# The states' keys through GpSimd's queue, and a start in which two blocks of tokens take the weights as they arrive

## The chip, the cores and the metric

The kernel runs on one core of a Trainium2 chip. The metric is the device time of one execution in microseconds (us), as the median of several runs. The core has five engines with a queue of instructions each: TensorE (PE, matrix products; its weight loads are shown apart as PEld), VectorE (DVE), ScalarE (ACT), GpSimd (POOL) and SyncE (SP), which here issues transfers only. ACT and POOL issue transfers too. An engine works through its queue in order; engines wait for each other by semaphores. Products go to PSUM, which has eight banks of 128 x 512 float32 values; everything else lies in SBUF or in memory.

## The reference, cut to what matters

One decoder layer on 1024 tokens of width 1024, all in float32:

```
xn   = rms_norm(x) * norm_mix_g
proj = xn @ w_in        # [sb_q, sb_k, sb_v, g_q, g_k, g_v, g_r, g_a, gate_sb, gate_gla]
o_sb  = stick_breaking_attention(sb_q, sb_k, sb_v)          # 8 heads x 64
o_gla = gla_chunked(g_q, g_k, g_v, log_a)                   # 4 heads, d_k 64, d_v 128
y = sigmoid(gate_sb + b0) * (o_sb @ w_branch_sb) + sigmoid(gate_gla + b1) * (o_gla' @ w_branch_gla)
h = x + y @ w_out
h = h + conv_ffn(rms_norm(h))                               # gated, causal convolution, width 2816
out = rms_norm(h) * norm_final_g
```

Two places concern the change. The first is the norm with the projection to `sb_v` (columns 1024 to 1535 of `w_in`), which is the first matrix product of the kernel. The second is the gated linear attention, whose state after each chunk is a sum of products of decayed keys with values:

```
k_to_end = kf * exp(cum_last - cum)
d_state  = einsum('bhnck,bhncv->bhnkv', k_to_end, vf)
state    = dec * state + d_state
```

## The kernel before, in words

Tokens are taken in eight blocks of 128 (`NT`), the width in eight pieces of 128 (`NK`). To keep float32's precision at a faster product, an operand is split into a high part (a cast to `fp32r` on ACT) and a low part (a subtraction on DVE); `split` (L118) does both, and a product of two operands is three products: high by high, low by high, high by low. `piece` (L180) splits a 128 x 512 piece of weights into one buffer.

Buffers come from rings: `t8` (16 of 8 KB a partition), `t4` (14 of 4 KB), `t2` (11 of 2 KB) and `bank` (the eight of PSUM). A new tile waits until an earlier one of its ring is given back. The program's order is a proposal: a planner puts the instructions of each engine into an order by their place in the program and by when it takes their operands and buffers to be ready. A dependency without a semaphore, added by hand (`add_manual_dep`), holds two instructions of one engine in an order.

**The start.** SP loads the first block of x (L383), the norm's factors broadcast to all 128 partitions (L396, 512 KB), then the weights of `sb_v` in four loads of two 128-row pieces each (L173), with the next blocks of x between them. `normed(0)` squares, scales (L310 to L313) and transposes (L321) block 0 and splits it; then the eight weight pieces are split; then for each block in turn `value` (L360) makes its 24 products (L367), copies the result (L372) and stores it (L373), while `normed` prepares the next block.

**The end of attention.** `attend` (L724) goes through the heads; its products (L677, L691) are mixed with steps of the gates' projection (`gates`, L555; products by `mac`, L197). `gather` (L706, products L712) finishes a head's two token blocks, its result goes to memory by SP (L720) and is loaded again by SP in `fetch_heads` (L702), added and split. After the loop `branch(0, ...)` (L910) is started: its first step loads the first weights of `w_branch_sb` and splits two pieces. Four steps of the gates follow (`BEFORE`, L991), then `fetch_rest` (L794) loads the decayed keys `kt_d`, which the kernel had stored earlier, in two loads of 512 KB on SP (L800), then the rest of the gates. Then `gated` (L885) runs the linear attention: `states` (L803) makes a product per chunk and pair of heads (L808), DVE adds it to the state (L815, L817) and POOL scales it (L819). Steps of `branch(0)`, which multiply the attention's rows by the branch's weights (`mac`, L197) and by the gates loaded on SP (L930), are set between them.

Of the kernel before, what the change touches and what calls it, by code (L numbers as in the profile page):

```python
# [34 lines left out]
C_GATE = 3088  # L35
T2 = 11
T4 = 14
FILL = 6, 4
# [10 lines left out]
FFN_FROM = 18  # L49
BEFORE = 4  # L50
PAIR_SKEW = 3
# [14 lines left out]
def block_kernel(ctx: ExitStack, tc: tile.TileContext, x, norm_mix_g, w_in, b_gate, w_alpha_up, b_alpha,  # L66
# [51 lines left out]
    def split(h, l, src):  # L118
        nc.scalar.copy(h, src)  # L119
        sub(l, src, h.bitcast(F32))  # L120


# [183 lines left out]

    def norm_rows(src, g, dst):

        ss, rs, ri = (cp.tile([P, 1], F32, tag=n, name=nm(n), bufs=2) for n in ("ss", "rs", "ri"))
        nc.scalar.activation(dst, src, AF.Square, accum_out=ss)  # L310
        nc.scalar.activation(rs, ss, AF.Sqrt, bias=eps, scale=1.0 / D)
        nc.vector.reciprocal(ri, rs)
        nc.vector.scalar_tensor_tensor(out=dst, in0=src, scalar=ri, in1=g, op0=ALU.mult, op1=ALU.mult)  # L313
# [45 lines left out]

    def value(ws, i, dst, after=None):  # L360
        pt = bank()
        t = slice((i % 4) * P, (i % 4 + 1) * P)
        for k in range(NK):
            xh, xl = xq[f"{i // 4 + 1}{k // 4 + 1}"]
            wh, wl = flat(ws[k])
            for m, (a, b) in enumerate(((xh, wh), (xl, wh), (xh, wl))):
                nc.tensor.matmul(pt, a[:, k % 4, t], b, start=k == 0 and m == 0, stop=k == NK - 1 and m == 2)  # L367
            if after is not None:
                ws[k] = wh = wl = None
                after(k)  # L370
        o = t2()
        nc.scalar.copy(o, pt)  # L372
        nc.scalar.dma_start(dst[i * P:(i + 1) * P, :], o)  # L373
# [11 lines left out]
    def normed(i):  # L385
        if i < NT:
            if i % 4 == 0:
                for kh in range(2):
                    xq[f"{i // 4 + 1}{kh + 1}"] = quarter()
            v = xs.pop(i)  # L390
            norm_rows(v[:, 0], gb, v[:, 1])
            turn(v[:, 1], i, xq)

    ws, ws2 = [], []
    fetch(0)
    nc.sync.dma_start(gb, norm_mix_g.to_broadcast([P, D]))  # L396
# [16 lines left out]

    for i in range(NT):
        fetch(i + 3)
        if i > 0:
            normed(i + 1)
        if i == 2:
            araw = load(w_in[:, C_GA:C_GA + RANK], NK, t2())
            aw = by(t2(F32R)[:, 0:2 * RANK * NK], NK)  # L420
            split(aw[:, :, 0:RANK], aw[:, :, RANK:], araw)
        if i == 4:
            vectors()
        value(ws, i, sbv_d, next_piece if i == NT - 1 else None)
        if i == 0:
            normed(1)
    for half in range(2):
# [347 lines left out]

    def after(b, a):
        tc.add_manual_dep(b.ins, a.ins.name,
                          mybir.DependencyInfo(mybir.DependencyClass.NoSync, mybir.DependencyReason.DATA),
                          reason="bank order")

    state, gv, gla = [], [], []
# [12 lines left out]
    def fetch_rest():  # L794
# [3 lines left out]
        for p in range(2):  # L798
            kt = t4()
            nc.sync.dma_start(kt, kt_d[p * P:(p + 1) * P, :])  # L800
            gla[p] += by(kt, NT), by(t4(), NT)
# [180 lines left out]
    for w in attend():  # L982
# [333 lines left out]
```

## Time and profile before

| | us |
|---|---|
| median of 3 runs | 1404.6 (1404.36 to 1404.93) |
| the profiled execution | 1404.87 |
| its span, first to last instruction | 1403.2 |
| PE busy | 1372.2 (98%) |
| DVE busy | 1063.9 (76%) |
| ACT busy | 643.6 (46%) |
| POOL busy | 128.8 (9%) |

The span is that of one execution taken by the hardware profiler, and times inside it count from its first instruction. The mean granted clock of TensorE is 0.996 of full speed. A line of the order of time has the start, the duration, the engine, the line of the kernel, the operation, the tile written and the tile read; in brackets stands how long the engine was idle before and what ended it. Several equal instructions in a row are merged ("x24"), and their duration is then that of the row.

### The profile page before, as it was taken

To read this page: it belongs to the slowest core of one execution; us is meant where nothing else is said; L and a number is where in the kernel's file an instruction comes from. 1 tells how busy PE (TensorE), PEld (TensorE's weight loads), DVE (VectorE), ACT (ScalarE), POOL (GpSimd) and SP (SyncE) were. 2 spreads that over 40 slices of the span, in tenths; PEclk is the share of its full clock that TensorE was granted. 3 is DMA by queue.
4 is the path that set the end of the run, shared out by engine and by line. 5 is a ranking of instruction groups with operands and counts; after the bars stand their busy time and mean duration, and the time that the engine had idled before them with its cause. 6 is when DMAs were issued, how large, how long until landed. Compare 5 with 4: busy or idle time off the path is not lost.

```text
span 1403.2 us, 18305 instructions
## 1 busy us (share of the span) xinstructions
PE 1372.2 (98%) x6549; PEld 1138.5 (81%) x6549; DVE 1063.9 (76%) x1640; ACT 643.6 (46%) x1242; POOL 128.8 (9%) x223
## 2 busy tenths in 40 slices
PE   7999999999999996999999999999999999999998
PEld 5788888888888875888888788888888888888886
DVE  6388788874878775648447997998888987897855
ACT  6234455653766563543234543333333333454654
POOL 0002133103011000300000000100000000000000
PEclk9999999999999998999999999999999999999999
DMA  6335277448766475464424434563554437953232
GB/s 241 139 97 167 70 231 247 143 157 231 194 150 152 127 223 196 148 213 158 155 91 135 114 96 150 190 217 134 180 181 150 152 108 267 324 176 99 97 106 105
DMA packets 165082, 228.44 MB, mean 163 GB/s; under 512 B 11017, under 2 KB 106379, under 8 KB 164480
## 3 DMA queue, kind: packets, MB, share of 16 engines
q1 hardware_dynamic: 136496, 141.63, 33.0%
q0 software_dynamic: 21920, 71.63, 15.6%
q10 hardware_dynamic: 6576, 14.03, 2.7%
q8 instruction: 51, 0.84, 0.3%
q14 instruction: 39, 0.32, 0.1%
HBM read 160.80 MB, written 66.45 MB: 162 GB/s over the span
## 4 chain that ended last, share of the span: by engine, by line
PE 56%; DVE 3%; DMA 1%; ACT 1%; issue 1%; SPq 0%; POOL 0%; ACTq 0%; DVEq 0%
PE bank L197 34%; PE bank L1179 15%; PE bank L1046 5%; DVE t L110 2%; DVE t L116 1%; DMA t<-kt_d 0%; PE bank L808 0%; DMA t<-gate_d 0%; PE bank L845 0%; DMA t<-in_w_branch_sb_dram 0%; DMA t<-in_w_branch_gla_dram 0%; PE bank L321 0%; PE bank L880 0%; SPq L702 0%; DVE t L313 0%
## 5 line engine op out<-in xcount | busy, mean ns | idle before, releaser
L197 PE MATMUL bank<-t,t 128*128 128x512 f32 x3624 | 862.9, 393 | 0.9 <-DVE t L110 0.8
L197 PEld LDWEIGHTS bank<-t,t 128*128 128x128 f32 x3624 | 677.1, 188 | 143.3 <-DVE t L110 1.6
L110 DVE TENSOR_TENSOR t<-t,t 128x512 fp32r<-128x512 f32 (+3 forms) x663 | 440.3, 697 | 93.9 <-ACT t L119 88.7
L119 ACT CAST t<-t 128x512 fp32r<-128x512 f32 x551 | 325.1, 626 | 342.1 <-DVE t L110 84.0
L116 DVE TENSOR_TENSOR t<-bank,t 128x512 f32<-128x512 f32 x266 | 179.3, 685 | 101.6 <-PE bank L197 58.3
L1179 PE MATMUL bank<-t,t 128*128 128x512 f32 x924 | 209.6, 389 | 0.0
L1179 PEld LDWEIGHTS bank<-t,t 128*128 128x128 f32 x924 | 173.4, 188 | 36.0
L110 DVE TENSOR_TENSOR t<-bank,t 128x512 fp32r<-128x512 f32 (+4 forms) x128 | 72.1, 578 | 33.2 <-ACT t L119 32.8
L367 PE MATMUL bank<-t,t 128*128 128x512 f32 x384 | 91.7, 398 | 1.6 <-ACT t L119 1.5
L1046 PE MATMUL bank<-t,t 128*128 128x512 f32 x384 | 88.9, 391 | 0.0
L116 DVE TENSOR_TENSOR t<-t,t 128x512 f32<-128x512 f32 x115 | 75.5, 685 | 15.8 <-ACT t L497 8.6
L367 PEld LDWEIGHTS bank<-t,t 128*128 128x128 f32 x384 | 72.9, 191 | 17.9 <-ACT t L119 2.2
L1077 ACT ACTIVATE t<-t,vcol 128x1024 f32<-128x1024 f32 x22 | 27.4, 1245 | 128.0 <-DVE t L116 128.0
L110 DVE TENSOR_TENSOR t<-t 128x512 f32<-128x512 f32 x120 | 82.1, 691 | 3.7 <-DMA t<-in_w_ffn_in_dram 3.3
L119 ACT CAST t<-bank 128x512 fp32r<-128x512 f32 (+3 forms) x124 | 61.8, 511 | 49.1 <-PE bank L691 27.3
L1046 PEld LDWEIGHTS bank<-t,t 128*128 128x128 f32 x384 | 71.6, 188 | 14.7
L1079 DVE SCALAR_TENSOR_TENSOR t<-t,vcol,t 128x1023 f32<-128x1023 f32 (+1 forms) x44 | 56.2, 1278 | 14.1 <-ACT t L1077 13.9
L682 DVE TENSOR_TENSOR_SCAN t<-t,t 128x128 f32<-128x128 f32 (+1 forms) x64 | 51.4, 814 | 14.4 <-ACT t L679 13.7
L691 PE MATMUL bank<-ident,t 128*128 128x128 f32 x288 | 53.5, 273 | 1.9 <-ACT t L588 1.3
L677 PE MATMUL bank<-t,t 128*128 128x128 f32 (+3 forms) x192 | 54.6, 368 | 0.1
L712 PE MATMUL bank<-t,t 128*128 128x256 f32 (+1 forms) x320 | 51.1, 276 | 0.4 <-DVE t L110 0.4
L712 PEld LDWEIGHTS bank<-t,t 128*128 128x128 f32 x320 | 46.4, 190 | 2.8 <-DVE t L110 0.6
(142 smaller groups left out, 760.4 us busy)
## 6 DMA issues: line engine op xcount, KB each, us to landing
t<-in_w_ffn_in_dram SPq DMA_DIRECT2D x50, 512.0 KB, 4.5
t<-in_w_in_dram SPq DMA_DIRECT2D x43, 512.0 KB, 5.8
act_d<-t POOLq DMA_DIRECT2D x22, 512.0 KB, 5.9
t<-in_w_ffn_out_dram SPq DMA_DIRECT2D x22, 512.0 KB, 7.1
wsum_d<-t POOLq DMA_DIRECT2D x22, 512.0 KB, 3.8
t<-act_d SPq DMA_DIRECT2D x22, 512.0 KB, 5.6
t<-wsum_d SPq DMA_DIRECT2D x44, 256.0 KB, 3.2
t<-in_w_ffn_out_dram SPq DMA_DIRECT2D x33, 256.0 KB, 2.6
```

The lines of the kernel that those rows point to most:

```text
L110: nc.vector.tensor_tensor(out=o, in0=a, in1=b, op=ALU.subtract)
L116: nc.vector.tensor_tensor(out=o, in0=a, in1=b, op=ALU.add)
L119: nc.scalar.copy(h, src)
L197: nc.tensor.matmul(pt, a[:, kk], b[:, kk], start=start and kk == 0 and m == 0, stop=stop and kk == k - 1 and m == 2)
L367: nc.tensor.matmul(pt, a[:, k % 4, t], b, start=k == 0 and m == 0, stop=k == NK - 1 and m == 2)
L677: nc.tensor.matmul(z[:, 0:w], q[:, a, e, ts_], kk[:, e, b0 * P:b1 * P], start=a == 0, stop=a == 1)
L682: nc.vector.tensor_tensor_scan(out=kr, data0=kr, data1=above[:, 0:w], initial=1.0, op0=ALU.mult, op1=ALU.max)
L691: nc.tensor.transpose(pt[:, b * P:(b + 1) * P], ke[:, b * P:(b + 1) * P], ident)
L712: nc.tensor.matmul(po[:, c0:2 * P], vt[b][:, head, :], a[b // 4][:, b % 4, c0:], start=(b == 0 and n == 0), stop=(b == nb - 1 and n == 1))
L1046: nc.tensor.matmul(pt, a[:, k % 4, t], b, start=(k == 0 and m == 0), stop=(k == NK - 1 and m == 2))
L1079: nc.vector.scalar_tensor_tensor(out=cv[:, i:], in0=av[:, :S - i], scalar=col(V_CW, (2 - i) * NF + f), in1=cv[:, i:], op0=ALU.mult, op1=AL ...
L1179: nc.tensor.matmul(pts[m][i], a[:, t], b, start=(k == 0 and x_ == 0), stop=(k == NH - 1 and x_ == 2))
```

## The change

The keys' two loads go to GpSimd's queue, and `fetch_rest` is called before the first step of `branch(0)`; the four gate steps between them fall away as a separate call, and are made by the call that makes the rest.

The start is written out by hand. The norm's factors are loaded as one row of 4 KB on ACT's queue and spread to all partitions by a product with a row of ones, into two PSUM banks; block 0 and block 1 are scaled from there, and the factors are copied to SBUF for the other blocks afterwards. Two idle products of the identity stand ahead of that product and four behind it. Blocks 0 and 1 are taken together: after each pair of weight pieces is split, the products with it are made for block 0 and, somewhat later, for block 1, into one bank each. The low parts of pieces 2, 3, 6 and 7 are made on GpSimd. `line` holds the listed instructions of ACT, DVE and GpSimd in the written order, and also the squares and reciprocals of the later blocks behind them.

```diff
+AWAKE = 2, 4
-BEFORE = 4
+    last = {}
+
+    def line(e, i):
+
+        if e in last:
+            after(i, last[e])
+        last[e] = i
...
+    grow, ones_row = t4(), t2()
+    nc.scalar.dma_start(grow[0:1], norm_mix_g)
+    nc.gpsimd.memset(ones_row[0:1, 0:P], 1.0)
     fetch(0)
-    nc.sync.dma_start(gb, norm_mix_g.to_broadcast([P, D]))
...
-    normed(0)
-    while raws:
-        raw = raws.pop(0)
-        ws += [piece(raw[:, n]) for n in range(2)]
+
+    def awake(n):
+        pt = bank()
+        for m in range(n):
+            nc.tensor.matmul(pt[:, 0:P], ident, ident, start=m == 0, stop=m == n - 1)
...
+    awake(AWAKE[0])
+    gps = [bank() for _ in range(2)]
+    for pt, c in zip(gps, COLS):
+        nc.tensor.matmul(pt, ones_row[0:1, 0:P], grow[0:1, c], start=True, stop=True)
+    awake(AWAKE[1])
...
+    def squared(i):
+        v = firsts[i]
+        ss, rs, ri = (cp.tile([P, 1], F32, tag=n, name=nm(n), bufs=2) for n in ("ss", "rs", "ri"))
+        line("a", nc.scalar.activation(v[:, 1], v[:, 0], AF.Square, accum_out=ss))
+        line("a", nc.scalar.activation(rs, ss, AF.Sqrt, bias=eps, scale=1.0 / D))
+        line("v", nc.vector.reciprocal(ri, rs))
+        for pt, c in zip(gps, COLS):
+            line("v", nc.vector.scalar_tensor_tensor(out=v[:, 1, c], in0=v[:, 0, c], scalar=ri, in1=pt,
+                                                     op0=ALU.mult, op1=ALU.mult))
...
+    def w_low(k):
+        l, a, h = lows.pop(k)
+        if k // 2 % 2:
+            line("p", nc.gpsimd.tensor_tensor(out=l, in0=a, in1=h.bitcast(F32), op=ALU.subtract))
+        else:
+            line("v", nc.vector.tensor_tensor(out=l, in0=a, in1=h.bitcast(F32), op=ALU.subtract))
...
+    def part(i, r):
+        t = slice(i * P, (i + 1) * P)
+        for m in range(3):
+            for k in (2 * r, 2 * r + 1):
+                x_, w = xq[f"1{k // 4 + 1}"][m == 1], flat(ws[k])[m == 2]
+                nc.tensor.matmul(pts[i], x_[:, k % 4, t], w, start=k == 0 and m == 0, stop=k == NK - 1 and m == 2)
+
+    squared(0)
+    turned(0)
+    w_high(0)
+    w_high(1)
+    w_low(0)
+    x_high(0, 0)
+    x_low(0, 0)
+    w_low(1)
+    part(0, 0)
+    w_high(2)
+    w_high(3)
+    w_low(2)
+    w_low(3)
+    x_high(0, 1)
+    x_low(0, 1)
+    squared(1)
+    part(0, 1)
+    w_high(4)
+    w_high(5)
+    w_low(4)
+    turned(1)
+    w_high(6)
+    w_high(7)
+    x_high(1, 0)
+    w_low(5)
+    x_low(1, 0)
+    part(0, 2)
+    part(1, 0)
+    w_low(6)
+    w_low(7)
+    part(1, 1)
+    x_high(1, 1)
+    x_low(1, 1)
+    part(0, 3)
+    value_out(pts[0], 0, sbv_d)
+    part(1, 2)
+    part(1, 3)
+    value_out(pts[1], 1, sbv_d)
+    for pt, c in zip(gps, COLS):
+        line("a", nc.scalar.copy(gb[:, c], pt))
...
-    for i in range(NT):
-        fetch(i + 3)
-        if i > 0:
-            normed(i + 1)
+    fetch(3)
+    normed(2)
+    for i in range(2, NT):
+        fetch(i + 2)
+        normed(i + 1)
...
             kt = t4()
-            nc.sync.dma_start(kt, kt_d[p * P:(p + 1) * P, :])
+            nc.gpsimd.dma_start(kt, kt_d[p * P:(p + 1) * P, :])
             gla[p] += by(kt, NT), by(t4(), NT)
...
+    fetch_rest()
     first_branch = branch(0, ob, w_branch_sb)
     fill(first_branch, 1)
-    fill(gate_steps, BEFORE)
-    fetch_rest()
     fill(gate_steps, 128)
```

`turned(i)` transposes the scaled block into two banks; `x_high` and `x_low` split half of it, `w_high` casts a weight piece. `part(i, r)` makes the six products of block i with weight pieces 2r and 2r + 1. `value_out` is the copy and the store of `value`, as before.

More of the change, by code (lines that the diff above doesn't have):

```diff
@@ L120, in split, with after @@
         sub(l, src, h.bitcast(F32))
+    def after(b, a):
+        tc.add_manual_dep(b.ins, a.ins.name,
+                          mybir.DependencyInfo(mybir.DependencyClass.NoSync, mybir.DependencyReason.DATA),
+                          reason="order")
     ident = cp.tile([P, P], F32, tag="ident", name="ident")
@@ L358, in block_kernel, with value_part @@
     gb = t4()
-    def value(ws, i, dst, after=None):
-        pt = bank()
+    def value_part(ws, i, ks, pt, after=None):
         t = slice((i % 4) * P, (i % 4 + 1) * P)
-        for k in range(NK):
+        for k in ks:
             xh, xl = xq[f"{i // 4 + 1}{k // 4 + 1}"]
@@ new lines, in block_kernel @@
+    pts = [bank() for _ in range(2)]
+    def part(i, r):
[14 more added lines that the diff above has]
+    w_high(2)
```

47 lines of the change are left out of this document (37 added, 10 removed).

## The prediction

> **What bounds the kernel.** I read the busy table first, then the busy time by stretch, and the list of waits for what stands in the holes.
>
> ```profile
> PE 1372.2 (98%) x6549; PEld 1138.5 (81%) x6549; DVE 1063.9 (76%) x1640; ACT 643.6 (46%) x1242; POOL 128.8 (9%) x223
> ...
> 0.00:20.00 20.00, 10.77 (x41) 8.27 (x41) 10.71 (x18) 12.93 (x26) 3.49 (x13) 1.00 0.91 340
> ...
> 90.00:520.00 430.00, 429.58 (x2207) 362.51 (x2206) 335.63 (x514) 236.35 (x465) 78.50 (x127) 1.00 0.62 174
> ...
> 530.00:545.00 15.00, 13.88 (x84) 11.83 (x82) 7.27 (x11) 4.94 (x12) 0.00 (x0) 1.00 0.30 92
> 545.00:555.00 10.00, 0.02 (x1) 0.05 (x1) 4.57 (x7) 3.02 (x5) 0.00 (x0) 0.65 0.86 304
> 555.00:585.00 30.00, 30.00 (x163) 24.65 (x164) 19.37 (x45) 12.13 (x39) 10.94 (x17) 0.95 0.59 198
> ```
>
> In a row of a stretch stand its length, the busy times of PE, weight load, DVE, ACT and POOL, the granted clock, the DMA share and GB/s. TensorE sets the time: in 90 to 520 us it rests 0.4 us of 430. Two holes remain that a change of order can reach: 9.2 us of the first 20, and practically the whole stretch 545 to 555. Whatever is won in them moves everything behind them forward, as PE has no other slack to absorb it. The waits name the second:
>
> ```profile
> PE bank L808 <- DMA t<-kt_d: 11.1, 1, 11.1
> ```
>
> **Part one: the states' keys.** The chain that ended last and the order of time around it:
>
> ```profile
> 547.88 6.97 DMA t<-kt_d
> 554.85 0.14 issue
> 554.98 1.19 PE bank L808 x2
> 556.17 2.41 PE bank L197 x6
> ...
> 559.44 1.39 PE bank L197 x6
> 560.83 0.43 PE bank L808 x2
> ```
>
> ```profile
> 533.87 1.18 PE L712 MATMUL bank<-t,t 128*128 128x256 f32 x9
> ...
> 538.02 0.54 SPq L173 DMA_DIRECT2D t<-in_w_branch_sb_dram  x1
> ...
> 540.66 3.21 PE L197 MATMUL bank<-t,t 128*128 128x512 f32 x13
> 542.07 0.62 ACT L119 CAST t<-t 128x512 fp32r<-128x512 f32 x1 [4.56 <-DMA t<-in_w_branch_sb_dram]
> ...
> 543.24 1.09 SPq L720 DMA_DIRECT2D osb_d<-t  x2
> 543.75 0.69 DVE L110 TENSOR_TENSOR t<-t,t 128x512 fp32r<-128x512 f32 x1 [0.34 <-ACT t L119]
> 544.42 3.41 SPq L702 DMA_DIRECT2D t<-osb_d  x7
> 547.88 1.03 SPq L800 DMA_DIRECT2D t<-kt_d  x2
> ...
> 552.32 1.46 DVE L110 TENSOR_TENSOR t<-t,t 128x512 fp32r<-128x512 f32 x2
> ...
> 555.07 0.69 DVE L110 TENSOR_TENSOR t<-t,t 128x512 fp32r<-128x512 f32 x1 [0.69 <-ACT t L119]
> ...
> 556.21 0.61 DVE L815 COPY t<-bank 64x128 f32<-64x128 f32 x2 [0.45 <-PE bank L808]
> ...
> 557.09 0.37 POOL L819 TENSOR_SCALAR t<-t,emid 128x128 f32<-128x128 f32 x1 [61.78 <-DMA t<-kt_d]
> ```
>
> The last gate products end at 540.66 + 3.21 = 543.87, and PE stands until 554.98: 11.11 us. The keys were stored to memory long before; their load is late only because it stands on SP behind the attention's last stores (L720) and its seven reloads (L702). On POOL nothing stands in front: its queue has been empty for 61.78 us when L819 runs. The pause also costs clock: the first state product takes 1.19 us where the same takes 0.43 at 560.83, and the first six branch products 2.41 against 1.39: 0.76 + 1.02 = 1.78. **The most that can be won is 11.11 + 1.78 = 12.9.** The Trainium skill ("TensorE: Matmul & The Clock Gate", Part 1) says that an idle window of about 3.4 us halves the clock and a busy one restores it; the two slow groups agree.
>
> When can the load start? It needs two buffers of the size-4 ring. The gather of the last head but one ends at 533.87 + 1.18 = 535.05 and gives back four. From there I take the issue, as POOL is free. Landing:
>
> ```profile
> t<-ki_d POOLq DMA_DIRECT2D x2, 512.0 KB, 7.7
> t<-kt_d SPq DMA_DIRECT2D x2, 512.0 KB, 7.0
> ```
>
> POOL's own 512 KB loads took 7.7 us: 535.05 + 7.7 = 542.8, before 543.87. Removed from SP are two issues (1.03 us), so the gate loads behind them go that much earlier; added to POOL are two issues that delay no one, as its next work, L819, needs the keys itself. The four gate steps that stood ahead of the fetch only stand elsewhere in the program: their products all come before the states either way, so they cost nothing.
>
> What is late next? The first branch block needs weight pieces that are ready at 543.75 + 0.69 = 544.44; one state product (0.43) covers most of it: 0.3 lost. Blocks of the second half need the attention's last four rows, ready at 552.32 + 0.69 = 553.0 and 555.07 + 0.69 = 555.8. Before them PE has four half blocks and seven state products, 4 x 1.39 + 7 x 0.43 = 8.6 us, so it gets there at about 553: in time. But PSUM has eight banks, and DVE, which empties them, is working through the adds and splits of those rows in order. After about 6.7 us (550.6) PE has filled them. If the states' copies (L815) stay behind the last split, as at 556.21 now, PE stands 5.9 us more and is cold again: 12.9 - 0.3 - 5.9 - 1.78 = 4.9 is won. If they slip in ahead, nothing is lost: 12.6. No row decides it. I take the place after the second row's split, 3.3 us of standing, short enough to leave most of the clock: 12.9 - 0.3 - 3.3 = **9.3** (4.9 to 12.6).
>
> **Part two: the start.**
>
> ```profile
> 1.26 0.42 SPq L396 DMA_DIRECT2D t<-in_norm_mix_g_dram  x1
> ...
> 4.75 1.06 ACT L310 ACTIVATE t<-t 128x1024 f32<-128x1024 f32 x1 [2.45 <-DMA t<-in_x_dram]
> ...
> 6.46 1.28 DVE L313 SCALAR_TENSOR_TENSOR t<-t,ri,t 128x1024 f32<-128x1024 f32 x1
> 7.86 1.14 ACT L119 CAST t<-t 128x512 fp32r<-128x512 f32 x2 [1.63 <-DMA t<-in_w_in_dram]
> ...
> 7.89 1.94 PE L321 MATMUL bank<-ident,t 128*128 128x128 f32 x8 [7.89 <-DVE t L313]
> ...
> 11.04 8.14 PE L367 MATMUL bank<-t,t 128*128 128x512 f32 x24 [1.21 <-ACT t L119]
> 11.99 0.62 ACT L119 CAST t<-t 128x512 fp32r<-128x512 f32 x1 [1.00 <-DMA t<-in_w_in_dram]
> ...
> 27.75 5.72 PE L367 MATMUL bank<-t,t 128*128 128x512 f32 x24
> ```
>
> ```profile
> 10.00:12.00 2.00, 0.83 (x2) 0.32 (x2) 1.89 (x3) 1.00 (x3) 0.00 (x0) 1.00 1.06 390
> ```
>
> Now block 0 starts at 11.04 and needs 8.14 us where a warm block needs 5.72, and block 2 starts at 27.75, with the transposes of four blocks done. Removed is the 512 KB broadcast of the norm's factors: at the 390 GB/s of that stretch 1.3 us for everything behind it, so the weights' casts can start at 6.55 (was 7.86) and 10.7 (was 11.99), the second pair likewise about 8.05. In its place stand a 4 KB row on ACT's queue, whose issue lies in the 2.45 us in which ACT waits for x, and two products that spread it. Their cost: a 256-wide state product takes 0.43 warm, so 512 wide 0.86, cold 1.7 each. If the row lands three us after ACT's first activation at 2.1, near the first x load less its bytes (4.75 - 0.81 of issue - 1.3), the first half of x is scaled at about 7.0 and not 6.46: 0.5 late.
>
> From there I go through the new written order with 0.57 for an ACT cast (1.14 for two), 0.69 for a DVE subtraction, 1.06 + 0.5 for a block's square and root, and 1.39 for a part of six products. ACT: casts 0 and 1 to 7.7, x high to 9.3, casts 2 and 3 to 10.4, x high to 11.0, block 1's square and root to 12.5, casts 4 to 7 to 14.8, block 1's x high to 15.6. DVE follows with the last x low of the first half of block 1 at 16.3. So PE has two thirds of block 0 done by 15.8 and then five parts that are its own bound: 5 x 1.39 = 7.0, end at 22.8, and 16 transposes (16 x 0.11 = 1.7, warm) for blocks 2 and 3: 24.5 against 27.75, **3.2 won**.
>
> ```profile
> L449 POOL TENSOR_TENSOR t<-t,t x9: 1289/1445/2896, 112.0 to 262.7; 128x512 f32<-128x512 f32 x9
> ```
>
> Four weight subtractions go to POOL at 1.45 each: two from 9.9 and two from 13.7 land by 16.7, before part (0,3) wants them at 18.6; at the worst 2.9 each the last is 1 us late. The idle products (six of 128 wide) lie in time in which PE has nothing; whether they warm it decides the parts until 15.8, which mostly wait for ACT anyway. By the page named above a window must be busy throughout, and six products would not fill one, though with the spreading they might. Were the clock still half at 15.8, two of the five parts would take twice 1.39: 2.8 lost, 0.4 won. Upper end: if the row is no bound and the transposes fall into PE's holes, 3.2 + 0.5 + 1.7 = 5.4. I take 3.2 (0.4 to 5.4).
>
> **Sum.** 9.3 + 3.2 = 12.5. The profiled execution took 1404.87 us, span 1403.2 within it; its time is 0.27 above the median. 1404.87 - 12.5 = 1392.4, on the median **1392.1**.
>
> **Rivals.**
> 1. *The gain row lands late.* Nothing of this size is loaded on ACT's queue at the start; on POOL's the small ones took long:
>
> ```profile
> t<-in_b_gate_dram POOLq DMA_DIRECT2D x1, 8.0 KB, 6.2
> ```
>
> Landing at 2.1 + 6.2 = 8.3 and a cold product put the scaling at 10.0, 3.5 us late, and the start wins nothing: 1404.6 - 9.3 = 1395.3. For: that row. Against: it was issued among five at once. Chance 0.12.
>
> 2. *The queue doesn't matter.* The keys' buffers come free only with the last gate product, and the load runs among the attention's reloads. Issue at 543.87 + 7.0 gives 550.9: 4.1 won there, 1404.6 - 4.1 - 3.2 = 1397.3. For: on SP the load stood even behind loads of a later stage. Against: four buffers at 535.05. Chance 0.10. The Trainium skill ("DMA: Bandwidth & Descriptors", Issuing engines are not separate DMA queues) says that all issuers share the same engines, so another issuer only saves issue time; with it alone the 3.4 us of L702 would be won. The share of 0.30 in 530 to 545 says that the engines had room.
>
> 3. *A new wait takes its place.* Keys now claim buffers ahead of the branch's first weights. If these get the keys' old place on SP, 547.88, they land 4.0 later (538.02 to 542.07) or up to 7.0; PE stands at the first branch block as long as now: nothing won there, 1404.6 - 3.2 = 1401.4. Against: four buffers come back at 535.05 and the second to last gate's before, so that the weights needn't wait for the keys' places. Chance 0.12.
>
> 4. *Slower.* The same claim, but the weights wait for buffers that states hold. Each us past 538.02 moves the pieces' cast, and behind it on ACT the last head's output, its store and reload. Up to 10.5 us PE only loses what it won, up to 13.7 the start's part too; from an issue past 551.7 on the kernel is slower, one us per us. An issue at 558 would give 1404.6 + 6.3 = 1410.9. Against: the last head's own four buffers come back by 541. Chance 0.06.
>
> **Chances.** Forecast 0.60, rivals 0.12, 0.10, 0.12, 0.06. The forecast's own ends are 12.6 + 5.4 = 18.0 and 4.9 + 0.4 = 5.3: 1386.6 to 1399.3, which holds rivals 1 and 2 as well (0.82); with tails on these I reach to rival 3's neighbourhood, 1401. Faster by over 0.2% (2.8 us, about what a measurement of this kernel can tell from no change): all of the first three cases and 0.08 of rival 3, 0.90; within 0.2%: 0.04; slower: 0.06.
>
> **What would show it.** Keys' two issues on POOL before 541 us on today's clock, landed before the last gate product ends; no PE wait on them in the list; first state product at 0.43. If PE's next hole ends on DVE's split of an attention row or a state copy, the 3.3 was right in kind; on a branch weight, rival 3. At the start: block 2's products near 24 us, ACT without holes from 6.6 to 15.6, scaling at about 7.0. I am wrong if PE is not bound behind 560, so that the shift is lost to gate loads.

## The result, and the profile after

| | before | after |
|---|---|---|
| median, us | 1404.76 (4 runs) | 1393.31 (1392.38 to 1393.54) |
| the profiled execution | 1404.87 | 1393.54 |
| its span | 1403.2 | 1391.8 |

The change made the kernel faster: the ratio is 0.9911 with a 95% interval of 0.9898 to 0.9923. The measured gain is 1404.76 - 1393.31 = 11.45 us; 12.5 was forecast.

Line numbers moved with the change. Of the lines used below, `mac` is now L202, the states' product L931, its copies L938, the transposes of the attention L819, `gather`'s products L840, the last head's output L846, its store L848, the reloads L830, the keys' load L923 and the gate loads L1053. In the start, L431 are the idle products, L440 the products that spread the norm's factors, L454 the scaling, L461 the transposes, L465 and L469 the high and low parts of x, L474 the casts of the weights, L480 and L482 their low parts on POOL and DVE, L491 the parts of blocks 0 and 1; L382 are the products from block 2 on. L716 is the activation of a finished gate, L968 a product of the linear attention that waits for POOL's L960. In the experiments' kernels the same lines can stand one or two higher or lower; e1 has the lines of before.

First the busy table of the kernel after, from its page:

```profile
PE 1376.2 (99%) x6565; PEld 1140.5 (82%) x6565; DVE 1064.1 (76%) x1638; ACT 645.1 (46%) x1244; POOL 133.4 (10%) x230
```

PE is busy 4 us longer than before in a span 11.4 us shorter: the start added the idle products (1.23 + 2.08 us) and the spreading (3.78). The busy time by stretch of the same kernel (length, then PE, weight load, DVE, ACT and POOL, granted clock, DMA share, GB/s) shows the two holes of before:

```profile
0.00:20.00 20.00, 18.06 (x63) 12.50 (x64) 10.18 (x14) 14.02 (x28) 9.16 (x17) 1.00 0.87 296
...
530.00:538.40 8.40, 8.40 (x59) 7.52 (x58) 3.67 (x6) 3.28 (x8) 1.07 (x2) 1.00 0.51 175
538.40:542.50 4.10, 1.58 (x9) 1.02 (x7) 0.01 (x1) 1.29 (x4) 0.00 (x0) 1.00 0.94 293
542.50:560.00 17.50, 17.49 (x88) 14.25 (x89) 14.52 (x31) 6.79 (x12) 5.30 (x10) 1.00 0.88 303
```

The hole of ten microseconds has become one of 4.10 - 1.58 = 2.5, in 538.4 to 542.5; there the DMA engines are at 0.94, where before they stood at 0.30 in 530 to 545. The first 20 us hold 18.06 us of PE work instead of 10.77. What ends the hole that is left stands in the list of PE's waits of the kernel after (total, times, longest); no wait on the keys is in it:

```profile
PE bank L202 <- ACT t L119: 2.5, 1, 2.5
...
PE bank L968 <- POOL t L960: 0.7, 1, 0.7
```

To measure how far the work behind the holes came forward I use one landmark, a row of 222 products that no wait breaks, some 67 us behind the second hole. From the chain that ended last, before and after:

```profile
621.51 50.35 PE bank L197 x222
```

```profile
535.88 5.88 DMA t<-in_w_branch_sb_dram
...
609.70 50.37 PE bank L202 x222
```

It starts 11.81 us earlier, and all but 0.4 us of that arrives at the end of the span. It divides at the last head but one, whose nine products started at 533.87: the order of time of the kernel after has them at 531.63. So 2.24 us were won at the start, and 11.81 - 2.24 = 9.57 at the keys.

```profile
531.63 1.17 PE L840 MATMUL bank<-t,t 128*128 128x256 f32 x9
...
533.36 1.11 POOL L923 DMA_DIRECT2D t<-kt_d  x2 [39.55 <-PE bank L819]
...
535.88 0.46 SPq L178 DMA_DIRECT2D t<-in_w_branch_sb_dram  x1
...
538.42 0.65 PE L931 MATMUL bank<-t,t 128*128 128x256 f32 x2
538.62 0.63 ACT L846 ACTIVATE t<-bank,t 128x128 f32<-128x128 f32 x2 [3.36 <-PE bank L840]
...
538.71 1.27 PE L202 MATMUL bank<-t,t 128*128 128x512 f32 x4
539.27 1.09 SPq L848 DMA_DIRECT2D osb_d<-t  x2
540.46 3.58 SPq L830 DMA_DIRECT2D t<-osb_d  x7
541.84 1.14 ACT L119 CAST t<-t 128x512 fp32r<-128x512 f32 x2 [2.60 <-DMA t<-in_w_branch_sb_dram]
...
542.51 0.73 PE L202 MATMUL bank<-t,t 128*128 128x512 f32 x2 [2.53 <-ACT t L119]
...
546.51 3.77 PE L202 MATMUL bank<-t,t 128*128 128x512 f32 x15
...
547.45 0.28 DVE L938 COPY t<-bank 64x128 f32<-64x128 f32 x1
...
549.01 0.69 ACT L716 ACTIVATE t<-bank,vcol 128x512 f32<-128x512 f32 x1 [0.82 <-PE bank L202]
```

The keys are issued at 533.36 and the first state product runs at 538.42, ahead of the last gate products. The planner no longer sets all thirteen of these together: four stand at 538.71, and nine are the first part of the row at 546.51, behind twelve branch products. The row's ninth product ends at 548.9, and the gate's activation on ACT, which needs the finished gate, starts at 549.01, in the middle of the row. What PE waits for now is the branch's first weights. They are issued at 535.88, while the keys are in flight, take 5.88 us instead of the 542.07 - 538.02 = 4.05 of before, and their cast ends the wait at 542.51. About 2.1 of the 2.53 us of this wait (nine products at 0.23) are no lost work: the gate products that now stand behind it stood in front before.

The start in the order of time:

```profile
2.92 3.78 PE L440 MATMUL bank<-t,t 1*128 1x512 f32 x4
...
6.04 1.44 DVE L454 SCALAR_TENSOR_TENSOR t<-t,ri,bank 128x512 f32<-128x512 f32 x2
...
6.62 2.08 PE L431 MATMUL bank<-ident 128*128 128x128 f32 x8
...
8.49 1.91 PE L461 MATMUL bank<-ident,t 128*128 128x128 f32 x8
...
10.23 4.56 PE L491 MATMUL bank<-t,t 128*128 128x512 f32 x13
...
10.78 2.97 POOL L480 TENSOR_TENSOR t<-t,t 128x512 fp32r<-128x512 f32 x2 [9.23 <-ACT t L474]
10.82 1.79 DVE L482 TENSOR_TENSOR t<-t,t 128x512 fp32r<-128x512 f32 x1
...
12.53 0.68 DVE L469 TENSOR_TENSOR t<-bank,t 128x512 fp32r<-128x512 f32 x1
...
14.64 2.38 DVE L482 TENSOR_TENSOR t<-t,t 128x512 fp32r<-128x512 f32 x2
14.71 3.47 POOL L480 TENSOR_TENSOR t<-t,t 128x512 fp32r<-128x512 f32 x2 [0.95 <-ACT t L474]
...
17.07 7.10 PE L491 MATMUL bank<-t,t 128*128 128x512 f32 x30 [0.25 <-DVE t L482]
...
25.68 5.90 PE L382 MATMUL bank<-t,t 128*128 128x512 f32 x24
```

The gain row is there at 2.92, and x is scaled at 6.04. The first half is scaled at about 6.04 + 0.72 = 6.76, yet its transposes start at 8.49: the idle products stand in front of them on PE. And one subtraction on DVE takes 1.79 where 0.69 was usual, just while POOL makes one of the same kind. Block 2 starts at 25.68.

### The profile page after: what moved, and what is told of

It is laid out like the page before. It is cut to its first block, busy times and chain, and to the rows that moved or that the text cites. A ratio compares the mean times of both kernels' runs of the same rounds, so it can differ in the third digit from the quotient of the medians.

```text
span 1391.8 us, 18351 instructions
## 1 busy us (share of the span) xinstructions
PE 1376.2 (99%) x6565; PEld 1140.5 (82%) x6565; DVE 1064.1 (76%) x1638; ACT 645.1 (46%) x1244; POOL 133.4 (10%) x230
## 4 chain that ended last, share of the span: by engine, by line
PE 58%; DVE 2%; DMA 1%; ACT 1%; issue 0%; SPq 0%; POOL 0%; ACTq 0%; DVEq 0%
PE bank L202 35%; PE bank L1301 15%; PE bank L1168 5%; DVE t L110 2%; DVE t L116 1%; PE bank L968 0%; DMA t<-in_w_branch_sb_dram 0%; PE bank L931 0%; DMA t<-gate_d 0%; PE bank L1003 0%; PE bank L337 0%; PE bank L955 0%; ACT t L119 0%; PE bank L980 0%; DVE t L329 0%
## 5 line engine op out<-in xcount | busy, mean ns | idle before, releaser
L202 PE MATMUL bank<-t,t 128*128 128x512 f32 x3624 | 861.9, 393 | 3.4 <-ACT t L119 2.5
L202 PEld LDWEIGHTS bank<-t,t 128*128 128x128 f32 x3624 | 676.1, 188 | 146.0 <-ACT t L119 3.5
L119 ACT CAST t<-t 128x512 fp32r<-128x512 f32 (+1 forms) x543 | 320.2, 626 | 319.8 <-DVE t L110 82.8
L1301 PE MATMUL bank<-t,t 128*128 128x512 f32 x924 | 209.6, 389 | 0.0
L1301 PEld LDWEIGHTS bank<-t,t 128*128 128x128 f32 x924 | 173.4, 188 | 36.0
L1168 PE MATMUL bank<-t,t 128*128 128x512 f32 x384 | 88.9, 391 | 0.0
L1168 PEld LDWEIGHTS bank<-t,t 128*128 128x128 f32 x384 | 71.6, 188 | 14.7
L382 PE MATMUL bank<-t,t 128*128 128x512 f32 x336 | 77.9, 391 | 0.0
L382 PEld LDWEIGHTS bank<-t,t 128*128 128x128 f32 x336 | 62.7, 188 | 13.1 <-DVE t L110 0.2
L819 PE MATMUL bank<-ident,t 128*128 128x128 f32 x288 | 53.4, 273 | 1.4 <-ACT t L716 0.8
L840 PE MATMUL bank<-t,t 128*128 128x256 f32 (+1 forms) x320 | 51.0, 276 | 1.0 <-DVE t L110 1.0
L840 PEld LDWEIGHTS bank<-t,t 128*128 128x128 f32 x320 | 46.4, 189 | 3.4 <-DVE t L110 1.2
```

Source lines behind the costliest of these rows:

```text
L202: nc.tensor.matmul(pt, a[:, kk], b[:, kk], start=start and kk == 0 and m == 0, stop=stop and kk == k - 1 and m == 2)
L819: nc.tensor.transpose(pt[:, b * P:(b + 1) * P], ke[:, b * P:(b + 1) * P], ident)
L840: nc.tensor.matmul(po[:, c0:2 * P], vt[b][:, head, :], a[b // 4][:, b % 4, c0:], start=(b == 0 and n == 0), stop=(b == nb - 1 and n == 1))
L1168: nc.tensor.matmul(pt, a[:, k % 4, t], b, start=(k == 0 and m == 0), stop=(k == NK - 1 and m == 2))
L1301: nc.tensor.matmul(pts[m][i], a[:, t], b, start=(k == 0 and x_ == 0), stop=(k == NH - 1 and x_ == 2))
```

## The experiments

Twelve kernels were run, in three groups of four, each group on one chip with the kernel before beside it (medians of before: 1405.21, 1405.49 and 1405.22). From the profiled execution of each come the start of block 2, the start of the last head but one's row of nine products ("gather"), the start of the landmark, and the time from the one to the other, in which the keys' part lies and the start does not.

| | median, us | ratio to before (95%) | block 2 | gather | landmark | between |
|---|---|---|---|---|---|---|
| before | 1404.76 | 1 | 27.75 | 533.87 | 621.51 | 87.64 |
| after | 1393.31 | 0.9911 (0.9898 to 0.9923) | 25.68 | 531.63 | 609.70 | 78.07 |
| e1_keys_only | 1395.81 | 0.9932 (0.992 to 0.9945) | 27.62 | 533.59 | 611.10 | 77.51 |
| e2_start_only | 1403.84 | 0.9987 (0.9977 to 0.9997) | 25.79 | 531.82 | 621.37 | 89.55 |
| e3_keys_sp_early | 1395.77 | 0.9935 (0.9922 to 0.9947) | 25.53 | 534.77 | 614.17 | 79.40 |
| e4_keys_pool_old_place | 1398.12 | 0.995 (0.9936 to 0.9963) | 25.52 | 531.95 | 614.22 | 82.27 |
| e5_no_idle | 1392.59 | 0.9906 (0.9893 to 0.992) | 24.32 | 530.37 | 608.75 | 78.38 |
| e6_idle_ahead_only | 1392.46 | 0.9905 (0.989 to 0.992) | 24.33 | 530.78 | 608.45 | 77.67 |
| e7_low_on_dve | 1392.86 | 0.9914 (0.99 to 0.9928) | 24.63 | 531.35 | 608.62 | 77.27 |
| e8_weights_pool_first | 1393.97 | 0.9916 (0.9902 to 0.9929) | 25.63 | 531.84 | 608.86 | 77.02 |
| e9_all | 1391.59 | 0.9901 (0.9887 to 0.9914) | 24.54 | 530.23 | 608.64 | 78.41 |
| e10_start_best | 1391.87 | 0.9906 (0.9892 to 0.9919) | 23.72 | 530.07 | 608.51 | 78.44 |
| e11_copies_on_act | 1391.42 | 0.9904 (0.9889 to 0.992) | 24.52 | 530.17 | 606.60 | 76.43 |
| e12_after_again | 1394.75 | 0.9928 (0.9916 to 0.9941) | 25.83 | 531.51 | 609.30 | 77.79 |

Medians of different groups are not compared to the last microsecond: the kernel after gave 1393.31 in one place and, as e12, 1394.75 in another. The stretch between differs too where nothing in it was changed: 78.07, 78.38, 77.67, 77.27 and 77.79 in after, e5, e6, e7 and e12. So a difference of less than one microsecond there is no finding, and even one of 1.4 needs a reason of its own: e8 and e9 have the same part of the keys, with 77.02 and 78.41. The wait on the branch's first weights scatters too: 2.53 us in after, and 1.6 in e12, the same kernel. The start of block 2 lies between 25.52 and 25.83 in after, e2, e3, e4, e8 and e12, which have the same start.

### The two parts by themselves

e1 is the kernel before with the keys' part alone:

```diff
-            nc.sync.dma_start(kt, kt_d[p * P:(p + 1) * P, :])
+            nc.gpsimd.dma_start(kt, kt_d[p * P:(p + 1) * P, :])
...
+    fetch_rest()
     first_branch = branch(0, ob, w_branch_sb)
     fill(first_branch, 1)
-    fill(gate_steps, BEFORE)
-    fetch_rest()
     fill(gate_steps, 128)
```

> The start of before, the keys' part of the change alone (GpSimd's queue, fetched ahead of the branch's first step). Theory: both traces run 2.2 us apart from block 2 on until 530 us, and 9.2 more after the keys, so the parts add: 1404.8 - 9.2 = 1395.6 (1394.5 to 1396.7). Rival: the start's lead is eaten or made by the end of attention; then this run lies below 1394 or above 1397.5.

Measured: 1405.21 - 1395.81 = 9.40 us won; between, 87.64 became 77.51. e2 is the kernel after with the keys on SP's queue at their old place, so the start alone:

```diff
-            nc.gpsimd.dma_start(kt, kt_d[p * P:(p + 1) * P, :])
+            nc.sync.dma_start(kt, kt_d[p * P:(p + 1) * P, :])
...
-    fetch_rest()
     first_branch = branch(0, ob, w_branch_sb)
     fill(first_branch, 1)
+    fill(gate_steps, BEFORE)
+    fetch_rest()
     fill(gate_steps, 128)
```

> The new start alone, the keys as before (SP's queue, after four gate steps). Theory: 1404.8 - 2.2 = 1402.6, with PE waiting about 11 us on the keys again. Rival: the start's 2.2 us do not come through the attention: 1404.8.

Measured: 1405.21 - 1403.84 = 1.4 us won; the interval of the ratio allows 0.4 to 3.2. The keys' part has the forecast size, and the start falls short. In e2's profiled execution block 2 starts 27.75 - 25.79 = 1.96 us earlier than before, the gather 533.87 - 531.82 = 2.05, but the landmark only 0.14. The rest is lost at the keys' hole, as PE's order of time in e2 shows:

```profile
553.54 1.19 PE L932 MATMUL bank<-t,t 128*128 128x256 f32 x2 [11.73 <-DMA t<-kt_d]
554.16 3.12 PE L203 MATMUL bank<-t,t 128*128 128x512 f32 x6
557.09 1.91 PE L932 MATMUL bank<-t,t 128*128 128x256 f32 x4
```

The first state product comes at 553.54 instead of 554.98, 1.44 early, and the pause before it has grown from 11.1 to 11.7. Behind it six products still take 3.12 us, and four state products 1.91; warm they take 1.75 and 1.02 in the other runs. TensorE's granted clock stays at half until 559.1 us in e2, 5.6 us past the first state product, and in before until 558.3, 3.3 us past it; at half clock this loses 1.1 us more, which with the longer pause is 1.7 of the 1.9 us that are missing. So a part of what the start wins is given back at a later wait while that wait exists. With the keys early it isn't, and the trace of after carries the start's 2.24 us up to the keys.

### Queue and place

Is the load late because of SP's queue, or because of its place in the program? e3 is the kernel after with the keys on SP, at the new place:

```diff
-            nc.gpsimd.dma_start(kt, kt_d[p * P:(p + 1) * P, :])
+            nc.sync.dma_start(kt, kt_d[p * P:(p + 1) * P, :])
```

> As after, but the keys on SP's queue, at their new place in the program. Theory (what stands ahead in the queue sets the landing): on SP they come behind the stores that wait for ACT until about 535.7, so two us later than on GpSimd's, and push the branch's first weights and the attention's reloads back by two issues; 2 to 4 us of the 9.2 are lost: 1395 to 1398. Rival (the queue does not matter, the place in the program does): as after, 1393.3. Rival (the place does not matter): 11 us of waiting are back, 1402.6.

e4 is the kernel after with the keys on POOL, at the old place:

```diff
-    fetch_rest()
     first_branch = branch(0, ob, w_branch_sb)
     fill(first_branch, 1)
+    fill(gate_steps, BEFORE)
+    fetch_rest()
     fill(gate_steps, 128)
```

> As after, but fetched at the old place in the program (after the branch's first step and four gate steps), on GpSimd's queue. Theory: the queue is what counts; the branch's first weights now claim their buffer ahead of the keys and land up to 2 us earlier, the keys later; PE's wait of 2.5 us on the branch's weights shrinks or is replaced by one on the keys: 1391.5 to 1395. Rival (the keys' claim on the buffers must come first): their load waits for the buffers of the last head, free about 538.6, and lands near 544 to 546: 1396 to 1399.

The three kernels and e2 have the same start, so the stretch between is compared with e2's 89.55. The place alone makes it 79.40 (10.2 us less), the queue alone 82.27 (7.3 less), both 78.07 (11.5 less). So the place does most: with it the queue adds 1.3 us, without it 7.3. Each of these is from one trace, and the 1.3 is little more than the scatter. The medians agree in order, 1403.84, then 1398.12 for the queue, 1395.77 for the place. e4's interval lies wholly above that of after and overlaps e12's by a little; e3's cannot be told from e12's.

e3's landmark, 614.17, would mislead here. In that execution the gather itself comes at 534.77, some 3 us later than in after, although PE's products stand in the same order up to the last head; its runs spread from 1393.78 to 1399.06, and the fastest of them is as fast as after. The trace shows where it was lost: PE waits 0.8 and 1.1 us at 360 us in the attention, and behind that the granted clock is at half for 3.4 us.

```profile
362.00:365.40 3.40, 3.40 (x13) 3.01 (x13) 2.96 (x6) 2.41 (x6) 0.00 (x0) 0.50 0.42 124
```

In the same stretch of after the clock is at 1.00, and PE starts 23 products instead of 13. Neither the keys nor their queue have a part in this.

SP's and PE's rows in e3:

```profile
538.92 1.04 SPq L923 DMA_DIRECT2D t<-kt_d  x2
...
540.06 0.38 SPq L178 DMA_DIRECT2D t<-in_w_branch_sb_dram  x1
...
542.92 0.67 PE L931 MATMUL bank<-t,t 128*128 128x256 f32 x2 [0.91 <-DMA t<-kt_d]
```

At the new place the keys stand ahead of the reloads on SP too and land at 542.9, so that the wait on them is 0.91 us, with twelve of the thirteen gate products still behind it. Counted from the gather, they go 538.92 - 534.77 = 4.15 us behind it, against 533.36 - 531.63 = 1.73 on POOL: that is what SP's queue still costs. In e4 the keys go at 534.87, early enough. What e4 loses is shown by ACT's and SP's rows:

```profile
534.87 1.11 POOL L924 DMA_DIRECT2D t<-kt_d  x2 [41.62 <-PE bank L820]
...
542.30 0.62 ACT L120 CAST t<-t 128x512 fp32r<-128x512 f32 x1 [6.72 <-DMA t<-in_w_branch_sb_dram]
542.82 0.62 ACT L847 ACTIVATE t<-bank,t 128x128 f32<-128x128 f32 x2
...
543.47 1.09 SPq L849 DMA_DIRECT2D osb_d<-t  x2
...
544.65 4.29 SPq L831 DMA_DIRECT2D t<-osb_d  x7
```

With the old place, ACT has the cast of the branch's first weights written ahead of the last head's output. It stands 6.72 us for those weights, and the output, finished on PE long before, stands behind it. With the new place the planner puts the output first (538.62 in after). So the store goes at 539.27 and not 543.47, and the reloads at 540.46 and not 544.65, 4.2 us earlier; e4's stretch between is 82.27 - 78.07 = 4.2 longer. That the two figures are equal is not a proof, but e4's waits fit: DVE comes late to the states' copies, since the attention's last rows come late. From 530 to 600 us PE waits 5.1 us in all, 1.9 more than in after, and from 556.2 to 559.6 the clock is at half, which costs about another 1.5.

```profile
PE bank L203 <- DVE t L939: 2.8, 1, 2.8
...
PE bank L932 <- ACT t L717: 1.1, 1, 1.1
```

Neither expectation for e4 holds: it is slower than the theory said, and it has the rival's time by another cause, as the keys were issued at 534.87 and no wait of PE is on them.

### The hole that is left

Theory: the wait on the branch's first weights is what remains. Rival: behind it stands the wait for a PSUM bank that the prediction named, and it takes the place. e8 sends these weights ahead of the keys, on POOL's queue:

```diff
-                    raws.append(load(w[:, i * P:(i + 2) * P], 4))
+                    q = nc.gpsimd if b == 0 and i == 0 else nc.sync
+                    raw = by(t4(), 4)
+                    q.dma_start(raw, w[:, i * P:(i + 2) * P].rearrange("(k p) c -> p k c", p=P))
+                    raws.append(raw)
...
-    fetch_rest()
     first_branch = branch(0, ob, w_branch_sb)
     fill(first_branch, 1)
+    fetch_rest()
```

> As after, but the branch's first weights are loaded on GpSimd's queue too, ahead of the keys. Theory: PE's remaining wait of 2.5 us at 540 is for these weights, which stand on SP behind the stores until 535.9 and then share the engines with the keys; on GpSimd's queue they are issued at about 533.4 and land near 538, so the wait goes and the clock's small loss with it: 2.0 to 2.8 us faster, 1390.5 to 1391.3. Rival: the keys, now behind, become the wait, or the attention's rows (ready 2 us later in the trace than PE needs them then): within 0.7 us of after.

Measured: 1393.97, no gain that can be told from after; the stretch between is 1.05 us shorter than in after and 0.77 shorter than in e12, about the size of its scatter. ACT's, DVE's and PE's rows in e8:

```profile
538.55 1.14 ACT L119 CAST t<-t 128x512 fp32r<-128x512 f32 x2 [3.07 <-DMA t<-in_w_branch_sb_dram]
...
538.63 3.21 PE L202 MATMUL bank<-t,t 128*128 128x512 f32 x13
...
551.26 0.68 DVE L116 TENSOR_TENSOR t<-t,t 128x512 f32<-128x512 f32 x1
...
551.97 0.29 DVE L938 COPY t<-bank 64x128 f32<-64x128 f32 x1
...
552.41 1.62 PE L202 MATMUL bank<-t,t 128*128 128x512 f32 x6 [1.99 <-DVE t L938]
```

The weights are cast at 538.55 instead of 541.84, and PE doesn't wait for them any more. It runs on until its banks are full, and then stands 1.99 us for a states' copy that DVE makes behind an addition of an attention row. The rival came: 2.5 us of one wait went, 2.0 of the next appeared. The thirteen gate products stand together again, at 538.63, ahead of the branch's. The same next wait shows beside the one on the weights in runs without this edit: 0.4 us in e12, 1.2 in e5 and 1.1 in e10.

e11 takes that next wait away as well. It is e9 (below: e8's edit together with the better start) with the first states' copies on ACT:

```diff
-                    nc.vector.tensor_copy(new[r], src)
+                    nc.scalar.copy(new[r], src)
```

> As the run before, with the first states' copies out of PSUM on ACT instead of DVE. Theory: PE's wait of 2.0 us is for a PSUM bank that DVE empties only at 552, behind adds that wait for the attention's rows; on ACT, which is idle then, the bank comes free by 546, and the wait goes: 1.0 to 2.0 us faster than the run before, with all waits of PE between 535 and 560 under 1 us in all. Rival (the later chunks' sums, also on DVE, hold the banks instead): the wait is named by L940 and stays at 1.5 to 2.

e9's list of PE's waits begins with 2.1 us for DVE's copy (its L936); in e11 that wait is gone, and only 0.8 us on another (DVE's L113) is left. The stretch between is 78.41 - 76.43 = 1.98 us shorter, but this isn't the wait alone. In e9's trace the clock is at half behind the wait:

```profile
552.30:555.70 3.40, 3.40 (x20) 2.49 (x19) 3.17 (x10) 1.41 (x3) 1.12 (x3) 0.50 1.05 368
```

That costs 1.7 us, and e8, with the same keys' part and a wait as long, has nothing of it. Against e8's 77.02 e11 is 0.6 shorter, inside the scatter. The medians, 1391.59 and 1391.42, show no gain either, where 1 to 2 us were expected. Whether the copies on ACT win anything stays open.

### The start

e5 leaves out all idle products, e6 only the four behind the spreading:

```diff
-    awake(AWAKE[0])
...
-    awake(AWAKE[1])
```

> As after, without any idle product. Theory: the four behind the spreading stand in the way of block 0's transposes, which now begin at 8.49 where their input is there at about 6.8; all that follows on ACT's written order comes 1.0 to 1.7 us earlier, and the clock, which is still low at 10 us in after, loses little: 0.5 to 1.7 us faster, 1391.6 to 1392.8. Rival: the idle products are what brings the clock up by 13 us; without them the parts run at half speed until 16 or later: 1 to 3 us slower, 1394.3 to 1396.3.

> As after, with the two idle products ahead of the spreading and without the four behind it. Theory: as without any, 1391.6 to 1392.8, and the transposes begin at about 6.9. Rival (the clock needs the four): 1394 or more.

Measured: block 2 at 24.32 in e5 and 24.33 in e6, 1.36 us before after's. PE's order of time in e6:

```profile
7.13 1.94 PE L460 MATMUL bank<-ident,t 128*128 128x128 f32 x8 [0.60 <-DVE t L453]
8.89 4.96 PE L490 MATMUL bank<-t,t 128*128 128x512 f32 x13
```

Without the four behind, the transposes start at 7.13, right after DVE's scaling, instead of 8.49: the same 1.36 us, and at the gather 1.26 (e5) and 0.85 (e6) of it are left. Whether the idle products warm anything isn't shown. The transposes take 1.94 us in e5 and e6 and 1.91 in after, where eight warm ones take 1.04 later on. The trace's record of the granted clock, which begins when the clock is up, begins at 12.6 us in after, at 12.2 in e5 and at 12.3 in e6. But in the six other runs with after's idle products it begins anywhere from 10.1 (e4) to 12.9 (e2), so that a gain of a microsecond could hide in it. Block 2 would have had little of it: 25.52 in e4, 25.79 in e2. The two idle products in front of the spreading neither help nor cost anything measurable. In the medians the 1.36 us can hardly be told from nothing: 0.9906 and 0.9905 against 0.9911, intervals overlapping.

e7 makes all low parts of the weights on DVE:

```diff
-        if k // 2 % 2:
+        if False:
```

> As after, with the low parts of the weight pieces 2, 3, 6 and 7 on DVE instead of GpSimd. Theory: GpSimd's subtractions take 1.5 to 1.7 us each and DVE's beside them 1.8 and 1.2 in place of 0.69, so DVE loses 1.6 us by them; moved, DVE gets four more at 0.69 = 2.8 in all, and part (0,1) has its low parts 1 us earlier: within 0.7 us of after, 1392.6 to 1394.0, with every subtraction at 0.69. Rival (DVE is the bound of the start): 1.2 to 2 us slower, 1394.5 to 1395.3.

Block 2 starts at 24.63, 1.05 us earlier than in after, though DVE has four instructions more. e10 joins e5's edit and e7's. DVE's group of these subtractions in the first 20 us (busy time, mean ns of one), in after and in e10:

```profile
L482 DVE TENSOR_TENSOR t<-t,t 128x512 fp32r<-128x512 f32 x4 | 4.9, 1234 | 0.0
```

```profile
L480 DVE TENSOR_TENSOR t<-t,t 128x512 fp32r<-128x512 f32 x8 | 5.1, 684 | 0.0
```

Eight of them without POOL take DVE 5.1 us, and four beside POOL 4.9. The low parts on POOL relieved DVE of 0.2 us.

> As after, with no idle product and all low parts of the weights on DVE; the keys' part as in after. Theory: the transposes again begin at about 7.1 and no subtraction meets GpSimd's, so block 2's products begin at 23.3 to 23.9 (25.68 in after) and the kernel is 1.6 to 2.4 us faster than after on the same chip. Rival (the start is bound by PE's own parts at the low clock): 24.3 as without the idle products alone, 1.2 to 1.4 us.

> The start of the run before, and the branch's first weights on GpSimd's queue ahead of the keys. Theory: the two waits at 540 and 549 (2.5 on the weights, or 2.0 on the states' copies in its place) are worth 0.5 to 1 us apart, so it lies 0 to 1 us below the run before. Rival: the reloads of the attention's rows are what both wait for; the same as the run before within 0.3.

> The changed kernel once more, beside the three others on one chip: 1392 to 1394.5, 0.991 of before. All theories expect the same; it is what the three are compared with.

e10, e9 and e12 (the kernel after, unchanged) ran on the same chip. e10 has block 2 at 23.72, 1.96 us before after's, as its theory had it, and a median of 1391.87. But e9 and e11, with the same start, have block 2 at 24.54 and 24.52, near the rival's 24.3. Their clock came up at 13.0 us and e10's at 11.7, and their first transposes began 0.3 us later; PE has no pause behind its transposes there, so a late clock costs time. So this start is worth 1.1 to 2.0 us at block 2. e9, which adds e8's edit, has a median of 1391.59, so e8's edit is worth nothing that can be measured here either. e12 gave 1394.75, a little more than expected. The three better kernels (e9, e10, e11) lie 2.9 to 3.3 us under it; e9's interval ends just below the beginning of e12's, and those of e10 and e11 overlap it slightly. In the traces e10's gather comes 1.44 us earlier than e12's and its landmark 0.79, so about two of its 2.9 us are not explained by them; e12's runs spread from 1393.42 to 1397.64, and the execution in the trace is the fastest of them, 1.1 us over e10's.

## Why the prediction was right, and where it wasn't

**What bounds the kernel.** Right. PE set the time, and 11.4 of the 11.81 us won at the landmark arrive at the end of the span.

**The keys' part: right in sum, by other terms.** 9.3 was forecast; 9.57 by the trace, and 9.40 alone in e1.

- *The hole goes, and the clock's loss with it.* Right. The keys went at 533.36, which is 535.60 with the start's 2.24 us added back, against 535.05 forecast; they took 5.0 us to land and not 7.7. No PE wait on them is left, and the first pair of state products takes 0.65 us where the same row takes 1.19 in e2. The 1.78 us for the clock were about right: in before it is at half for 3.3 us of PE's work, which loses 1.7.
- *The branch's first weights, 0.3.* Mis-sized: 2.53, and 1.6 in e12. The step let them land at the old time, in 4.05 us. The keys' megabyte is in flight with them, and they took 5.88, in e12 5.0. The greater part is the order of the gate products: the step had all thirteen in front of the weights, and nine, 2.1 us, stand behind them now. In e4, where thirteen stand in front, the wait is 0.6, with the weights cast as late as 542.30. Rival 3 named these weights, but with another mechanism and the whole hole as its price. e8 shows the wait to be theirs: sent ahead of the keys they are cast 3.3 us earlier, and the wait is gone.
- *3.3 us of standing on full PSUM banks.* Not in after's trace, though the mechanism is real. The nine gate products fill PE's time in just this place, and one state product had come earlier, so that the states' banks were asked for later; DVE's first copy at 547.45 was in time. In e12, the same kernel, 0.4 us of it came, and with the weights' wait removed, in e8, 1.99, ended by the copy behind DVE's work on an attention row, as the step had it.
- *The sum.* A third term was put at nothing: 0.65 us at 594.05, where PE waits for POOL's L960; before has no such wait. So 12.9 - 2.53 - 0.65 = 9.7 us are left, and 9.57 came. Against the forecast the errors are +2.2, -3.3 and +0.65. The first two belong together, as the nine products that lengthen one wait shorten the other; that all three nearly cancel is luck.
- *"Late only because it stands on SP", and the four gate steps "cost nothing".* This is the step that failed. Of the 11.5 us between e2 and after, the place alone brings 10.2 and the queue alone 7.3. What held the keys was read rightly, the stores and reloads in front of them; that they needed another queue to get past these was not. The place puts the keys ahead of SP's reloads whatever the queue, and it decides the order on ACT, where the last head's output stood behind the weights' cast: the stores and reloads behind it come 4.2 us earlier, which is what e4 lacks. The prediction saw that order only inside rival 4, as a danger.

**The start: right in direction, 1 us too much.** 3.2 forecast, 2.24 by the trace, 1.4 alone (0.4 to 3.2). Block 2 came at 25.68 and not at 24.5.

- *The gain row.* It was used 2.1 us after its issue at 0.81; the forecast had it at about 5. Scaling began at 6.04, so that its first half was done before 7.0. Rival 1 did not come.
- *The idle products "lie in time in which PE has nothing".* This failed. The four behind the spreading stood ahead of the transposes of data that was there 1.7 us earlier; e5 and e6 give 1.36 us for it, more than the whole shortfall at block 2 (25.68 - 24.5 = 1.2). That they might not warm the clock was said; the runs show no gain by them, and can't rule out one of a microsecond.
- *Four low parts on POOL at 1.45 each.* Two took 2.97 and two more 3.47 us, inside the 2.9 each that the step allowed. Left out altogether was what they do to DVE beside them; e7 gives 1.05 us for it at block 2.
- *Parts at the warm rate from 15.8.* About right. In after 30 products take 7.10 us from 17.07 on, 0.24 each.

**The rivals.** Rival 2 (the queue doesn't matter) fails as it was put: the buffers were free long before the last gate product, and at the old place the queue is worth 7.3 us. At the new place it is nearly true, with 1.3. Rival 4 did not come: the weights were issued at 535.88, before the first state product. The sign "PE is not bound behind 560" came in a small way, with the 0.65 us at 594.05.

## What to carry to other kernels

A load that comes late has more than one thing in front of it: look for the queue on which it is issued, and for its place in the program, which sets the order on other engines too; then try each alone, because here the two overlapped (10.2 and 7.3 us alone, 11.5 together), and the one that the change was named for was the smaller. A wait that is removed lets the next one show, as e8 and e11 did one after the other, so follow PE past the first hole and price the second. A wait's length isn't its cost: look for work that has moved behind it, as the nine gate products did here. Work that is meant to fill idle time must not stand in an in-order queue in front of work that may come sooner than thought.

## What the runs showed of the hardware

**POOL slows DVE on SBUF operands.** A DVE subtraction of two 128 x 512 SBUF operands took 0.68 us alone, and 1.79, and then 2.38 for two, while POOL made the same kind of subtraction. In the same stretch DVE's subtractions with one operand in PSUM kept their duration: 0.68 at 12.53. The Trainium skill ("SBUF — State Buffer", Who interferes with whom) says that a DVE instruction with two SBUF inputs contends with GpSimd, and one with at most one doesn't; the trace agrees.

**The clock of the start isn't in the granted clock's column.** The column reads 1.00 in the first 20 us, but the trace's record of the clock has no row before 12.6 us in after and before 15.6 in before, and begins there at full. What the clock was until then, the products tell: in after they start 0.43 us apart until 12.1 and 0.23 from 13.0 on, and eight transposes take 1.91 us that take 1.04 later. In after PE has work from 1.60 us on almost without a pause, in e5 only from 2.33 on with pauses, and in before only from 7.89. The six other runs with after's idle products came up to speed between 10.1 and 12.9.

**A short wait can cost the clock.** In e3 waits of 0.8 and 1.1 us within 3 us were followed by 3.4 us at half clock, in e9 one of 2.06; in after one of 2.53 and in e8 one of 1.99 were not. Why one tips it and the other doesn't stays open here.

**A product with a one-row operand isn't cheap at the start.** Spreading the row's two halves of 512 took 3.78 us of PE at the low clock, about what the prediction's cold bound of 1.7 each gave (3.4).
